# One of seven products of a SwiGLU block: high and low tokens side by side in matmuls of 512 columns, for eight of ten weight pairs

## The chip, the cores and the metric

The kernel runs on one core of a Trainium2 chip. Its engines are named as the profile names them: PE (matmuls; PEld is its weight load), DVE (VectorE), ACT (ScalarE), POOL (GpSimd) and SP (SyncE, which here issues DMAs). The metric is the device time of one execution in microseconds (us); less is better.

## The reference

One hybrid block on 512 tokens of width 1024, all in float32. A first normalisation and input product feed two token mixers (a gated convolution and a gated linear recurrence), which are merged by sigmoid gates. Then follows the channel mixer, in which the change lies:

```
h = rmsnorm(x, norm2_g[l])
x = x + (jax.nn.silu(h @ ffn_w1[l]) * (h @ ffn_w3[l])) @ ffn_w2[l]
return rmsnorm(x, norm_f_g)
```

The hidden width is 2816, so `ffn_w1` and `ffn_w3` are 1024x2816, and `ffn_w2` is 2816x1024.

## The kernel before

**Precision.** PE multiplies in a reduced format, so each float32 operand is split into a high and a low part (`split_to`, L121): ACT casts the value to the high part (L123), and DVE or POOL subtracts it from the value, which gives the low part (L119). A product is then three matmuls: high by high, high by low, low by high.

**Seven products.** For the channel mixer the tokens and the weight matrices are cut in quarters, and seven products of sums of quarters take the place of eight of quarters. The 22 column blocks of `ffn_w1` and `ffn_w3` are treated as 11 pairs `k`. Pair 0 is done plainly, pairs 1 and 2 (`FIRST`) and 3 and 4 (`NEXT`) are begun early, the others run through. In the order of `F_ORDER` (L404) a pair has the products `b11`, `t1`, `b21`, `t2`, `b22`, `t3`, and `t4` of a pair comes after `t2` of the next one; for pairs 1 to 4 `b11` and `b21` are done ahead. The token side of `t1` is called `s1`: for each of the four chunks of 128 of the contraction, the left half (`LO`, columns 0 to 255) of two tiles `hs0_0h` and `hs0_0l` and their like (the profile writes `hs_0h`, `hs_0l`).

**One product.** `f_product` (L1073) takes the weights of both matrices as eight blocks of 128x128, high and low. Matrix 1 goes to the columns `LO` of one bank of 512 columns, matrix 3 to the columns `HI` (256 to 511). Per matrix and chunk there are three matmuls of 256 columns (L1080), 24 in all.

**What follows a product.** `ffn_product` (L1169) writes `t1` to a bank `fe` out of a pool of two banks, and ACT copies it to a tile `se` in SBUF (L1185, 128x512). Later DVE adds `se` to the bank of `b22` (L906), and the product `t3` to `se`; ACT's silu (L1145) and a multiply on DVE (L1146) make the inputs `ou`, `ov` of the output product (`or`, L953). For `t2` ACT copies the running sum to a second bank first (L1180).

**The weights.** SP loads quarters of the raw weights (`f_load`, L345, two DMAs of 256 KB each, one for each matrix) into a pool of four raw buffers or into a second pool for those that sums are made in. The sums for `t1`, `t2` and `t3` are made on DVE (L357, and L119 for the difference); the one for `t4` is made by a DMA that accumulates, issued by POOL (L355). Each is then split by ACT and DVE into one of five buffers `hl_...` (a name `hl_ft` stands for `t1` to `t4`, `hl_fb` for `b11` to `b22`). Splits are put into the program four ahead of the product that uses them (`AHEAD`). SP issues in order, so a load that waits for its buffer holds all that are behind it.

**Tiles and order.** Most tiles of 128x512 come out of one set of 59 slots (`longt`, `SLOTS`). A scheduler puts the program in its order and sets the waits; PE runs its matmuls in the order of the code.

Of the kernel before, what the change touches and what calls it, by code (L numbers as in the profile page):

```python
# [8 lines left out]
F32 = mybir.dt.float32  # L9
F32R = mybir.dt.float32r  # L10
# [34 lines left out]
PLAIN, FIRST, NEXT = 0, (1, 2), (3, 4)  # L45
# [41 lines left out]
def tile_block(ctx, tc, a, out):  # L87
    nc = tc.nc
# [8 lines left out]
    def tiles(tag, bufs):  # L97
        p_ = pool(tag, bufs)
        return lambda name, dtype=F32: p_.tile([P, T], dtype, tag=tag, name=name)

    longt, shortt, gatet = tiles("long", SLOTS), tiles("short", SHORT), tiles("gate", GATES)
# [5 lines left out]
    def bank(name):  # L107
        return psum.tile([P, T], F32, tag="mm", name=name)

    def bank2(name):  # L110
        return psum2.tile([P, T], F32, tag="cv", name=name)

    vec, act, pe, pool_e = nc.vector, nc.scalar, nc.tensor, nc.gpsimd
# [66 lines left out]
    def emit_to(n, copy=act.copy, lo_by=None):  # L180
        while emitted[0] < min(len(chunks), n):
            emit_chunk(copy, lo_by)

    def weights(key, ahead=AHEAD):
        i = next(i for i, c in enumerate(chunks) if c[0] == key)
        emit_to(i + 1 + ahead)
        return held.pop(key)
# [409 lines left out]
    HALVES = [slice(0, 256), slice(256, 512)]  # L597
# [293 lines left out]
    for j in range(8):  # L891
        ws = w_tiles(f"lo{j}_0", 5) + w_tiles(f"lo{j}_1", 5)
        ps = bank(f"yb{j}")
# [12 lines left out]
    add = lambda o, x, y: vec.tensor_tensor(out=o, in0=x, in1=y, op=ALU.add)  # L906
    LO, HI = HALVES
# [99 lines left out]
    for n, j in enumerate(mixq.order()):  # L1007
        ws = w_tiles(f"co{j}", ND)
        ps = bank(f"ya{j}")
# [64 lines left out]
    def f_product(ps, k, x_, w_, again=False, ahead=AHEAD):  # L1074

        h, l = weights(f"f{w_}_{k}", ahead)
        for i in range(2):
            for c, (xh, xl) in enumerate(x_):
                for m, (lw, rx_) in enumerate(((h, xh), (h, xl), (l, xh))):
                    pe.matmul(  # L1080
                        ps[:, HALVES[i]], lw[:, 4 * i + c, :], rx_, start=not (again or i or c or m),
                        stop=bool(i and c == 3 and m == 2), skip_group_check=True,
                    )

    first = {}
    for k in FIRST:
        first[k] = bank(f"fr1_{k}"), bank(f"fr2_{k}")
# [10 lines left out]
    with tc.manual_schedule(engines={ET.PE}):  # L1098
        ws = w_tiles(f"f1_{PLAIN}", ND, 0)
        for q in range(4):  # L1100
            cs, ks = HALVES[q // 2], range(4 * (q % 2), 4 * (q % 2) + 4)
# [8 lines left out]
    f_in = {n: [] for n in ("a11", "a12", "a22", "s1", "s2", "s3", "s4")}  # L1110
# [32 lines left out]
    def f_out(c, dst, sign=1.0):  # L1143
        s_ = shortt("sl")
        act.activation(s_[:, LO], c[:, LO], AF.Silu, scale=sign)  # L1145
        vec.scalar_tensor_tensor(out=dst, in0=c[:, HI], scalar=sign, in1=s_[:, LO], op0=ALU.mult, op1=ALU.mult)  # L1146
# [15 lines left out]
    for k in NEXT:  # L1162
        f_product(first[k][1], k, f_in["a12"], "b21", True)
        o7.uv[k] = longt(f"ou{k}"), longt(f"ov{k}")
        f_out(first[k][1], o7.uv[k][0][:, LO])

    seven = {}

    def ffn_product(n, k):  # L1169

        b_ = seven.setdefault(k, {"a": first[k][0]} if k in BEGUN else {})
        x_ = {"b11": "a11", "b21": "a12", "b22": "s4", "t1": "s1", "t2": "s2", "t3": "s3", "t4": "a22"}[n]
        r = {"b11": "a", "b21": "b", "b22": "a", "t1": "e", "t2": "a", "t3": "c", "t4": "c"}[n]
        if n in ("b11", "t1"):
            b_[r] = (bank2 if r == "e" else bank)(f"f{r}_{k}")
        ps = b_[r]
        f_product(ps, k, f_in[x_], n, n not in ("b11", "t1"))
        if n in ("b11", "t2"):
            new = b_["b" if n == "b11" else "c"] = bank(f"f{n}_{k}")
            act.copy(new, ps)  # L1180
            if n == "b11":
                o7.uv[k] = longt(f"ou{k}"), longt(f"ov{k}")
        elif n == "t1":
            b_["se"] = shortt(f"se_{k}")
            act.copy(b_["se"], ps)  # L1185
        elif n == "b22":
            add(ps, ps, b_["se"])
        elif n == "t3":
            newest["added"] = add(b_["se"], ps, b_["se"]).ins
        if n not in ("b11", "t1", "t2"):  # L1190
            i, cs = {"b21": (0, LO), "b22": (0, HI), "t3": (1, HI), "t4": (1, LO)}[n]
            f_out(b_["se"] if n == "t3" else ps, o7.uv[k][i][:, cs], -1.0 if n in ("b22", "t3") else 1.0)
        if n == "t4" and k >= SUMS_FROM:
            o7.pair(k - SUMS_FROM)

    for n, k in F_ORDER:
        ffn_product(n, k)
# [93 lines left out]
```

## Time and profile before

| | |
|---|---|
| time, median of 3 runs | 797.41 us (797.23 to 797.61) |
| time of the profiled execution | 797.7 us |
| its span, first to last instruction | 795.9 us |
| granted TensorE clock | 1.000 |
| stage in which the ten pairs' products are computed | about 496 to 682 us |
| output product and end | 682 to 796 us |

The span begins with the first instruction and ends with the last, so 1.8 us of the profiled execution lie around it. A row of a timeline has a start, a duration, the engine, the line of the code, the operation, what is written and read, and in brackets how long the engine stood idle ahead of it and what ended that. Durations of DVE and ACT rows overlap the next row's start by a little; the distance of two starts is what one costs its engine. A row of a table of windows has the stretch, its length, the busy time of PE, PEld, DVE, ACT and POOL with the number of instructions, the granted clock, the busy share of the DMA engines, and GB/s. A row of waits has the waiting engine, its line, what ended the wait, the time in all, how many there were, and the longest.

### The profile page before, as it was taken

To read this page: it belongs to the slowest core of one execution; us is meant where nothing else is said; L and a number is where in the kernel's file an instruction comes from. 1 tells how busy PE (TensorE), PEld (TensorE's weight loads), DVE (VectorE), ACT (ScalarE), POOL (GpSimd) and SP (SyncE) were. 2 spreads that over 40 slices of the span, in tenths; PEclk is the share of its full clock that TensorE was granted. 3 is DMA by queue.
4 is the path that set the end of the run, shared out by engine and by line. 5 is a ranking of instruction groups with operands and counts; after the bars stand their busy time and mean duration, and the time that the engine had idled before them with its cause. 6 is when DMAs were issued, how large, how long until landed. Compare 5 with 4: busy or idle time off the path is not lost.

```text
span 795.9 us, 12177 instructions
## 1 busy us (share of the span) xinstructions
PE 789.2 (99%) x4369; PEld 690.5 (87%) x4369; DVE 673.2 (85%) x1020; ACT 471.7 (59%) x683; POOL 228.8 (29%) x181
## 2 busy tenths in 40 slices
PE   9999999999999999999999999999999999999997
PEld 8888888888888888888888898999999999888885
DVE  6699899999989988786787889978878887889757
ACT  6646585987768855563335575545455555577443
POOL 1855766797666856030000000000000000000000
PEclk9999999999999999999999999999999999999999
DMA  6945646487555664368847545566555553676652
GB/s 213 257 130 143 187 144 208 121 247 208 173 168 173 213 182 120 128 203 263 276 160 243 172 134 158 131 171 181 155 133 133 133 133 106 210 258 207 198 173 106
DMA packets 184604, 140.29 MB, mean 176 GB/s; under 512 B 14259, under 2 KB 162143, under 8 KB 184543
## 3 DMA queue, kind: packets, MB, share of 16 engines
q1 hardware_dynamic: 183103, 134.27, 55.2%
q0 software_dynamic: 1440, 5.24, 3.5%
q8 instruction: 34, 0.56, 0.3%
q14 instruction: 27, 0.22, 0.1%
HBM read 113.79 MB, written 18.64 MB: 166 GB/s over the span
## 4 chain that ended last, share of the span: by engine, by line
PE 99%; DVE 0%; issue 0%; ACT 0%
PE z L534 36%; PE or L953 13%; PE ft L1080 7%; PE yb L534 7%; PE fa L1080 7%; PE fr L1080 6%; PE ya L534 5%; PE mxr L953 5%; PE fe L1080 4%; PE g L827 3%; PE fb L1080 2%; PE f L534 2%; PE warm L506 1%; PE f L1106 1%; PE tx L574 1%; PE th L574 0%
## 5 line engine op out<-in xcount | busy, mean ns | idle before, releaser
L702 DVE SCALAR_TENSOR_TENSOR cv<-u,par,cv 128x511 f32<-128x511 f32 (+19 forms) x240 | 162.4, 730 | 5.0 <-ACT cv L699 4.7
L119 POOL TENSOR_TENSOR hl_in<-raw_in,hl_in 128x1024 fp32r<-128x1024 f32 x51 | 123.5, 2426 | 83.1 <-ACT hl_in L123 69.6
L355 POOL DMA_DIRECT2D raw_fb<-raw_fb x10 | 8.7, 874 | 298.4 <-DVE raw_fb L357 186.1
L119 POOL TENSOR_TENSOR ows<-ows 128x256 f32<-128x256 f32 x66 | 56.7, 861 | 37.7 <-DMA ows<-in_ffn_w_dram 34.7
L123 ACT CAST hl_ft<-raw_fb 128x1024 fp32r<-128x1024 f32 x40 | 41.8, 1048 | 32.5 <-DVE raw_fb L357 17.0
L123 ACT CAST hl_in<-raw_in 128x1024 fp32r<-128x1024 f32 x50 | 52.1, 1043 | 10.4 <-PE z L534 6.6
L119 DVE TENSOR_TENSOR hl_ft<-raw_fb,hl_ft 128x1024 fp32r<-128x1024 f32 x40 | 48.5, 1220 | 7.0 <-ACT hl_ft L123 6.9
L119 DVE TENSOR_TENSOR hl_fb<-raw_fb,hl_fb 128x1024 fp32r<-128x1024 f32 x30 | 36.6, 1221 | 9.5 <-ACT hl_fb L123 9.3
L357 DVE TENSOR_TENSOR raw_fb<-raw_fb,raw_fb 128x1024 f32<-128x1024 f32 x20 | 24.5, 1225 | 20.3 <-DMA raw_fb<-in_ffn_w_dram 20.0
L534 PE MATMUL z<-h10h,hl_in 128*128 128x512 f32 (+1 forms) x108 | 41.5, 385 | 0.0
L534 PE MATMUL z<-h17h,hl_in 128*128 128x512 f32 (+1 forms) x108 | 41.1, 381 | 0.0
L534 PE MATMUL z<-h13h,hl_in 128*128 128x512 f32 (+1 forms) x108 | 41.1, 381 | 0.0
L534 PE MATMUL z<-h15h,hl_in 128*128 128x512 f32 (+1 forms) x108 | 41.1, 381 | 0.0
L534 PE MATMUL z<-h14h,hl_in 128*128 128x512 f32 (+1 forms) x108 | 41.1, 381 | 0.0
L534 PE MATMUL z<-h16h,hl_in 128*128 128x512 f32 (+1 forms) x108 | 41.1, 381 | 0.0
L534 PE MATMUL z<-h12h,hl_in 128*128 128x512 f32 (+1 forms) x108 | 41.1, 381 | 0.0
L534 PE MATMUL z<-h11h,hl_in 128*128 128x512 f32 (+1 forms) x108 | 41.1, 381 | 0.0
L123 ACT CAST hl_fb<-raw_fb 128x1024 fp32r<-128x1024 f32 x30 | 31.4, 1047 | 8.9 <-PE mxr L953 3.7
L119 DVE TENSOR_TENSOR hl_ob<-raw_ob,hl_ob 128x1024 fp32r<-128x1024 f32 (+1 forms) x23 | 27.0, 1174 | 11.0 <-ACT hl_ob L123 10.9
L123 ACT CAST hl_ob<-raw_ob 128x1024 fp32r<-128x1024 f32 (+1 forms) x23 | 23.3, 1015 | 21.6 <-PE or L953 10.8
L1080 PE MATMUL fe<-hs_0h,hl_ft 128*128 128x256 f32 x160 | 30.7, 283 | 0.0
L1080 PE MATMUL ft<-hs_1h,hl_ft 128*128 128x256 f32 x160 | 30.4, 283 | 0.0
(1016 smaller groups left out, 2610.0 us busy)
## 6 DMA issues: line engine op xcount, KB each, us to landing
raw_in<-in_w_in_dram SPq DMA_DIRECT2D x52, 512.0 KB
raw_fb<-in_ffn_w_dram SPq DMA_DIRECT2D x96, 256.0 KB
ows<-in_ffn_w_dram SPq DMA_DIRECT2D x44, 256.0 KB
os<-ows SPq DMA_DIRECT2D x22, 512.0 KB
raw_ob<-in_ffn_w_dram SPq DMA_DIRECT2D x33, 256.0 KB
raw_ot<-os SPq DMA_DIRECT2D x33, 256.0 KB
raw_lo<-in_lru_w_out_dram SPq DMA_DIRECT2D x16, 320.0 KB
raw_fb<-raw_fb POOLq DMA_DIRECT2D x10, 512.0 KB, 4.6
```

Of the source, the lines that this page charges most:

```text
L119: return eng.tensor_tensor(out=o, in0=x, in1=y, op=ALU.subtract)
L123: copy(h, full)
L355: pool_e.dma_start(out=q, in_=y, accum_op=ALU.add)
L357: vec.tensor_tensor(out=q, in0=q, in1=y, op=ALU.add)
L506: pe.matmul(wp[:, :P], ones, ones, start=True, stop=True)
L534: pe.matmul(ps, l, r, start=i == 0, stop=i == n - 1)
L574: pe.transpose(ps[:, t * P : (t + 1) * P], src, ident)
L702: vec.scalar_tensor_tensor(out=acc[c][:, s:], in0=u[c][:, : T - s], scalar=dw(c, s), in1=acc[c][:, s:], op0=ALU.mult, op1=ALU.add)
L827: pe.matmul(ps, l, r, start=k == 0, stop=k == len(mms) - 1)
L953: pe.matmul(banks[i], l_[:, ts], r_, start=start and n == 0, stop=stop and n == 2, skip_group_check=again)
L1080: pe.matmul(ps[:, HALVES[i]], lw[:, 4 * i + c, :], rx_, start=not (again or i or c or m), stop=bool(i and c == 3 and m == 2), skip_group_c ...
L1106: pe.matmul(plain_1[:, cs], l, r, start=k == 0 and m == 0, stop=k == ND - 1 and m == 2)
```

## The change

A new function `f_wide` does the product `t1` of the pairs 3 to 10 (those not in `FIRST`). For it the high and the low part of `s1` are put side by side, once, in four tiles `s1b` of 512 columns, by eight DMAs from SBUF to SBUF. Each matrix has a bank of its own: a matmul of 512 columns multiplies the high weights with both parts at once, and one of 256 columns adds the low weights times the high tokens to the left half. The two halves of a bank must then be added: ACT copies the left half of each bank into its half of `se`, and DVE adds the right half.

```
+    def f_wide(banks, k, x_, both_, w_):
+
+        h, l = weights(f"f{w_}_{k}")
+        for i, ps in enumerate(banks):
+            for c, (xh, _) in enumerate(x_):
+                pe.matmul(ps, h[:, 4 * i + c, :], both_[c], start=c == 0, stop=False, skip_group_check=True)
+                pe.matmul(ps[:, LO], l[:, 4 * i + c, :], xh, start=False, stop=c == 3, skip_group_check=True)
...
+    s1_both = [longt(f"s1b{c}", F32R) for c in range(4)]
+    for both_, parts_ in zip(s1_both, f_in["s1"]):
+        for cs, v in zip(HALVES, parts_):
+            nc.sync.dma_start(both_[:, cs].bitcast(F32), v.bitcast(F32))
...
+        if n == "t1" and k not in FIRST:
+            wide = [bank2(f"fe{i}_{k}") for i in range(2)]
+            f_wide(wide, k, f_in[x_], s1_both, n)
+            b_["se"] = shortt(f"se_{k}")
+            for cs, ps in zip(HALVES, wide):
+                act.copy(b_["se"][:, cs], ps[:, LO])
+                add(b_["se"][:, cs], ps[:, HI], b_["se"][:, cs])
+            return
```

On PE the rows of `t1` of pair 3 began before with these (a name is followed by a number of its own; `x2` stands for two like rows on end; one matrix has 12 matmuls of this kind, the product 24):

```order
L1080 MATMUL fe_5172<-hs_0h,hl_ft_3_5048 128x256
L1080 MATMUL fe_5172<-hs_0l,hl_ft_3_5048 128x256
L1080 MATMUL fe_5172<-hs_0h,hl_ft_3_5048 128x256 x2
L1080 MATMUL fe_5172<-hs_0l,hl_ft_3_5048 128x256
L1080 MATMUL fe_5172<-hs_0h,hl_ft_3_5048 128x256 x2
```

In the changed kernel the same place has a first bank (5184) with eight rows and a second (5185) that begins like it:

```order
L1090 MATMUL fe_3_5184<-s1b_4868,hl_ft_3_5060 128x512
L1091 MATMUL fe_3_5184<-hs_0h,hl_ft_3_5060 128x256
L1090 MATMUL fe_3_5184<-s1b_4869,hl_ft_3_5060 128x512
L1091 MATMUL fe_3_5184<-hs_0h,hl_ft_3_5060 128x256
L1090 MATMUL fe_3_5184<-s1b_4870,hl_ft_3_5060 128x512
L1091 MATMUL fe_3_5184<-hs_0h,hl_ft_3_5060 128x256
L1090 MATMUL fe_3_5184<-s1b_4871,hl_ft_3_5060 128x512
L1091 MATMUL fe_3_5184<-hs_0h,hl_ft_3_5060 128x256
L1090 MATMUL fe_3_5185<-s1b_4868,hl_ft_3_5060 128x512
```

Twenty-four rows of 256 columns became sixteen, of 512 and 256 in turn; the products ahead and behind have the rows that they had, and so has PE everywhere else.

On SP, these are the loads of raw weights for pairs 2 and 3 before:

```order
L345 DMA raw_fb_2_4878<-in_ffn_w_dram 128x4x128 x2
L345 DMA raw_fb_2_4872<-in_ffn_w_dram 128x4x128 x2
L345 DMA raw_fb_2_4875<-in_ffn_w_dram 128x4x128 x2
L345 DMA raw_fb_3_5035<-in_ffn_w_dram 128x4x128 x2
L345 DMA raw_fb_3_5038<-in_ffn_w_dram 128x4x128 x2
```

And in the changed kernel (`raw_fb_3_5047` is the quarter `b11` of pair 3, `raw_fb_3_5050` the quarter `b12`, in which the sum is made):

```order
L345 DMA raw_fb_2_4887<-in_ffn_w_dram 128x4x128 x2
L1178 DMA s1b_4868<-hs_0h 128x256
L1178 DMA s1b_4868<-hs_0l 128x256
L1178 DMA s1b_4869<-hs_0h 128x256
L1178 DMA s1b_4869<-hs_0l 128x256
L1178 DMA s1b_4870<-hs_0h 128x256
L1178 DMA s1b_4870<-hs_0l 128x256
L1178 DMA s1b_4871<-hs_0h 128x256
L1178 DMA s1b_4871<-hs_0l 128x256
L345 DMA raw_fb_3_5047<-in_ffn_w_dram 128x4x128 x2
L345 DMA raw_fb_3_5050<-in_ffn_w_dram 128x4x128 x2
```

The eight copies stand between the last load for pair 2 and the first for pair 3; all other rows of SP keep their order.

On DVE, around `t1` of pair 5 before (`hl_fb_5` is the split for `b22` of pair 5, `hl_ft_5` that for its `t3`, `raw_fb_6` the sum for `t1` of pair 6):

```order
L1146 TENSOR_SCALAR ov_4864<-se_5367,sl 128x256
L119 TENSOR_TENSOR hl_fb_5_5539<-raw_fb_5_5404,hl_fb_5_5539 128x1024
L357 TENSOR_TENSOR raw_fb_6_5601<-raw_fb_6_5601,raw_fb_6_5598 128x1024
L119 TENSOR_TENSOR hl_ft_5_5568<-raw_fb_5_5369,hl_ft_5_5568 128x1024
L1146 TENSOR_SCALAR ou_5536<-fb_5_5534,sl 128x256
```

And in the changed kernel:

```order
L1154 TENSOR_SCALAR ov_4864<-se_5368,sl 128x256
L119 TENSOR_TENSOR hl_fb_5_5544<-raw_fb_5_5408,hl_fb_5_5544 128x1024
L906 TENSOR_TENSOR se_5563<-fe_5_5542,se_5563 128x256
L357 TENSOR_TENSOR raw_fb_6_5601<-raw_fb_6_5601,raw_fb_6_5598 128x1024
L906 TENSOR_TENSOR se_5563<-fe_5_5543,se_5563 128x256
L119 TENSOR_TENSOR hl_ft_5_5568<-raw_fb_5_5373,hl_ft_5_5568 128x1024
L1154 TENSOR_SCALAR ou_5540<-fb_5_5538,sl 128x256
```

The add of the first bank stands ahead of the next pair's sum, the add of the second ahead of the split for `t3`. Pairs 5 to 9 look like this. For pairs 3, 4 and 10 both adds stand together, behind the split for `t3` in pairs 3 and 4. In the rows of pairs 8 to 10 some rows of DVE and ACT that make the sums for the output product also change places.

## The prediction

> **What bounds the kernel now.** I read the page from the top: busy shares, the clock row, then the chain that ended last.
>
> ```profile
> PE 789.2 (99%) x4369; PEld 690.5 (87%) x4369; DVE 673.2 (85%) x1020; ACT 471.7 (59%) x683; POOL 228.8 (29%) x181
> PEclk9999999999999999999999999999999999999999
> PE 99%; DVE 0%; issue 0%; ACT 0%
> ```
>
> PE is busy for 99% of the span, at full clock in all forty slices, and it is 99% of the chain. Only work taken from PE, or a wait put in front of it, can move the end. Next I read the table of windows over the stretch in which the eight changed products lie (k = 3 to 10, from 532 to 682 us), and the waits from 505 to 690.
>
> ```profile
> 532.00:682.00 150.00, 150.00 (x1252) 150.00 (x1251) 118.47 (x151) 78.87 (x115) 6.01 (x7) 1.00 0.53 141
> DVE raw_fb L357 <- DMA raw_fb<-in_ffn_w_dram: 20.0, 9, 3.3
> PEld ft L1080 <- DVE se L906: 0.3, 1, 0.3
> PEld fr L1080 <- ACT ft L1180: 0.2, 1, 0.2
> ```
>
> In these 150 us PE is never idle. DVE is busy for 118.47, ACT for 78.87, and the DMA engines for 0.53 of the time. PE waits only twice between 505 and 690, 0.3 and 0.2 us. DVE waits 20.0 us for raw weights, so it has room too.
>
> **What a matmul costs.** The chain of waits lists whole runs of equal matmuls, so a spacing is a quotient.
>
> ```profile
> 375.34 43.52 PE ya L534 x192
> 584.10 2.88 PE fe L1080 x24
> ```
>
> 192 matmuls of 512 columns take 43.52 us: 226.7 ns each. 24 of 256 columns, one `fe` product, take 2.88 us: 120.0 ns each. Twice 120.0 is 240.0, so a pair of 256 with the same weights costs 13.3 ns more than one of 512. If a matmul is a constant plus its columns, 106.7 ns stand for 256 columns and 13.3 for the instruction. I take that reading, since 106.7 x 2 + 13.3 gives the 226.7 back.
>
> The wide product puts 512 and 256 columns in turn. The timeline has two unstalled places where the size changes:
>
> ```profile
> 458.61 0.39 PE L953 MATMUL mxr<-mxt43h,mxvb3l 128*128 128x512 f32 x1
> 458.84 0.28 PE L1080 MATMUL fr<-h20h,hl_fb 128*128 128x256 f32 x1
> 458.96 0.28 PE L1080 MATMUL fr<-h20l,hl_fb 128*128 128x256 f32 x1
> ...
> 685.66 0.28 PE L1080 MATMUL ft<-h27h,hl_ft 128*128 128x256 f32 x1
> 685.78 0.40 PE L953 MATMUL or<-hl_ob,ous0h 128*128 128x512 f32 x1
> ```
>
> From 512 to 256 the starts are 0.23 apart, from 256 to 256 and from 256 to 512 0.12: no extra cost for the change of size, to the 10 ns of this column.
>
> [...]
>
> **PE's part of the change.** Per product 24 x 120.0 = 2.88 us become 8 x 226.7 + 8 x 120.0 = 2.77 us: 0.107 us less. There are eight products: **0.85 us** (64 x 13.3 ns). PE's order is otherwise the same.
>
> **The eight copies on SP.** Each fills 128x256 of a long tile from `hs_0h` or `hs_0l`. They stand behind the loads for k = 2 and ahead of those for k = 3. The rows below are from SP's timeline, the waits of its queue, the page's list of DMA issues, a table of windows, and DVE's timeline.
>
> ```profile
> 67.85 0.54 SPq L807 DMA_DIRECT2D ext1h<-xb2h  x1
> 69.72 0.60 SPq L807 DMA_DIRECT2D ext3l<-xb2l  x1
> SPq L345 <- DMA raw_fb<-raw_fb: 10.2, 1, 10.2
> raw_fb<-raw_fb POOLq DMA_DIRECT2D x10, 512.0 KB, 4.6
> 505.00:511.00 6.00, 6.00 (x53) 6.00 (x52) 4.41 (x7) 1.99 (x4) 0.00 (x0) 1.00 0.88 260
> 511.00:515.00 4.00, 4.00 (x34) 3.83 (x33) 3.93 (x4) 2.50 (x4) 0.86 (x1) 1.00 0.03 8
> 515.00:518.50 3.50, 3.50 (x31) 3.50 (x31) 3.50 (x5) 1.52 (x3) 0.00 (x0) 1.00 0.79 150
> 522.15 1.23 DVE L357 TENSOR_TENSOR raw_fb<-raw_fb,raw_fb 128x1024 f32<-128x1024 f32 x1 [2.85 <-DMA raw_fb<-in_ffn_w_dram]
> ```
>
> Issuing: the existing copies of one tile into another, of the same 128 KB, hold SP 0.54 to 0.60 us each (four from 67.85 to 70.32, 0.62 apart), so eight take about 5 us. The `b11` loads of k = 3, which are among those of the first window, go that much later, and SP comes to its wait at 513 instead of 508. The queue had nothing else to do: SP waits 10.2 us at that place (508 to 518) for POOL's accumulating DMA. Transfer: 8 x 128 KB = 1.05 MB. At the 260 GB/s at a share of 0.88 of the first window (295 at full share) that is 3.6 us of all DMA engines. The DMA engines stood at 0.03 from 511 to 515, which is 3.9 us of room. So the copies and the moved load fit, by a little, ahead of the accumulate, which moves 512 KB from 515 to 518.5 and whose landing releases the next load. The moved load itself is a summand of the sum that DVE starts at 522.15, several microseconds behind its landing. The first wide product starts at 532.1, some 18 us after the copies land. Cost between nothing and the full 3.6 us of delay on the weights for k = 3 and 4; I take nothing, and the second rival prices the rest.
>
> **ACT and DVE.** One ACT copy of 128x512 becomes two of 128x256 and two DVE adds of 128x256. Their timelines around k = 5:
>
> ```profile
> 566.85 0.59 ACT L1185 COPY se<-fe 128x512 f32<-128x512 f32 x1 [0.73 <-PE fe L1080]
> 563.47 0.68 DVE L906 TENSOR_TENSOR se<-ft,se 128x512 f32<-128x512 f32 x1
> 564.06 0.42 DVE L119 TENSOR_TENSOR oe<-ou,ov 128x256 f32<-128x256 f32 x1
> 564.40 1.22 DVE L119 TENSOR_TENSOR hl_ft<-raw_fb,hl_ft 128x1024 fp32r<-128x1024 f32 x1
> 570.34 1.23 DVE L357 TENSOR_TENSOR raw_fb<-raw_fb,raw_fb 128x1024 f32<-128x1024 f32 x1 [2.97 <-DMA raw_fb<-in_ffn_w_dram]
> 574.17 1.22 DVE L119 TENSOR_TENSOR hl_ft<-raw_fb,hl_ft 128x1024 fp32r<-128x1024 f32 x1
> ```
>
> ACT's pass over 512 columns takes 0.59 us, so two over 256 take between 0.59 and 1.18; I take 0.7, as on DVE two passes over 256 (0.34 each, below) cost a little more than one over 512 (0.59), and ACT has 71 idle us in the window for eight times the difference. By the next start, a DVE pass over 256 takes 0.34; no add of this shape from PSUM to SBUF stands in the trace, so it is bounded by 0.34 and by 0.59, the 512 add (563.47 to 564.06). I take 0.34: 0.68 us per pair, 5.4 us in all, on an engine with 31 idle us in the window. For k = 5 to 9 the first add stands ahead of the next pair's sum. At k = 5 that sum waits 2.97 us for its load until 570.34, and the add can run at about 567.5: hidden. The second delays the split behind it by 0.34. The weights for `t1` of k = 6 are begun at 574.17 and done at 575.4, and PE reads them at 584.10, so 0.7 us on DVE are covered by 8.7. Without that cover PE would lose all of them, 5.4 us.
>
> For k = 3 and 4 both adds stand behind the `t3` split. Here the cover is thinnest:
>
> ```profile
> 537.50 1.23 DVE L357 TENSOR_TENSOR raw_fb<-raw_fb,raw_fb 128x1024 f32<-128x1024 f32 x1 [3.26 <-DMA raw_fb<-in_ffn_w_dram]
> 538.80 1.05 ACT L123 CAST hl_ft<-raw_fb 128x1024 fp32r<-128x1024 f32 x1 [3.04 <-DVE raw_fb L357]
> 539.76 0.58 ACT L1180 COPY ft<-fr 128x512 f32<-128x512 f32 x1
> 540.73 0.28 PE L1080 MATMUL fr<-hs_1h,hl_fb 128*128 128x256 f32 x1
> 538.98 2.36 DVE L119 TENSOR_TENSOR hl_ft<-raw_fb,hl_ft 128x1024 fp32r<-128x1024 f32 x2
> 546.49 0.28 PE L1080 MATMUL fe<-hs_0h,hl_ft 128*128 128x256 f32 x1
> ```
>
> The sum for k = 4 waits 3.26 us for its load, ACT's cast waits for the sum, and the copy that frees `fr` for `b22` of k = 3 is queued behind the cast. It ends at 540.34, PE needs it at 540.73: 0.39 us of cover, of which the faster product eats 0.11. No add comes ahead of this. The two adds of k = 3 go between the two splits from 538.98, the second of which is for `t1` of k = 4: it ends at 542.0 instead of 541.3, and PE reads it from 546.5 on. In the tail (k = 8 to 10) four more long slots are held and DVE's rows change places, one `ov` write now behind `b11` of k = 10 on PE; the split for `b22` of k = 10 shows the cover there:
>
> ```profile
> 666.34 1.23 DVE L119 TENSOR_TENSOR hl_fb<-raw_fb,hl_fb 128x1024 fp32r<-128x1024 f32 x1 [0.96 <-ACT hl_fb L123]
> 676.09 0.28 PE L1080 MATMUL fa<-hs_1h,hl_fb 128*128 128x256 f32 x1
> ```
>
> It is done at 667.6 and read from 676.09: 8.5 us, and I charge nothing. The output stage is started by PE's last `t4`, so the gain passes through.
>
> **The sum.** The profiled execution took 797.7 us, a span of 795.9 and 1.8 around it. 797.7 - 0.85 = 796.85. The median of the runs shown is 797.41, 0.3 lower, so on that scale **796.6 us**, 0.11% less. A measurement of this kernel tells about 0.2% from no change: 1.6 us, so "faster" is under 795.8 and "slower" over 799.0.
>
> **Rivals.** 1) *The 13.3 ns are not the instruction's.* If they go with columns, or if alternating two output widths pays them back, the products stay at 2.88 us: 797.3 to 797.5. For it speaks that no run in the trace alternates unstalled. Against it stand the two changes of size above. That the change doesn't do what it says comes out at the same time.
>
> 2) *Slower: the copies delay the weights of k = 3 and 4.* Should they collide with the accumulate by x us, the load behind it, the sum at 537.50, the cast and the copy that frees `fr` all come x later, and PE waits x - 0.28 at 540.73. It breaks even with the gain at x = 1.1; it is slower by over 0.2% from x = 2.7 (2.4 lost against 0.85 gained). With all of the 3.6 us serial it is 796.6 + 3.3 = 799.9. For it: the sums at 522.15 and 537.50 both end waits for their loads, so a delay of the loads reaches them whole. Against it: the hole of 3.9 us, at the same place.
>
> 3) *Slower: alternation stalls.* There is one place where 512 and 256 alternate:
>
> ```profile
> 477.36 0.40 PE L534 MATMUL f<-h20l,hl_f 128*128 128x512 f32 x1
> 477.59 0.38 PE L1106 MATMUL f<-h26h,hl_f 128*128 128x256 f32 x1
> 477.80 0.39 PE L534 MATMUL f<-h21h,hl_f 128*128 128x512 f32 x1
> 478.04 0.39 PE L1106 MATMUL f<-h26l,hl_f 128*128 128x256 f32 x1
> ```
>
> Here a 256 is followed only after 0.21 instead of 0.12. At 64 places that would be 64 x 0.09 = 5.8 us lost: 802.3. But those 256s read `h26h` and `h26l` just as they are made (their 0.38 and 0.39 against 0.28 elsewhere shows the wait), which the wide product's inputs are not.
>
> **How the numbers follow.** Forecast (0.85 gained, all else hidden): 0.66, 796.2 to 797.0. Rival 1, or a collision that eats the gain: 0.21, 797.0 to 799.0. Rivals 2 and 3 beyond 0.2%: 0.05 and 0.05. More than forecast: 0.03. The range runs from 796.2 to 798.0: 0.4 below for run-to-run spread, above past the case without gain. Faster by over 0.2% needs 1.6 us where PE's whole saving is 0.85: 0.03. Within: 0.87. Slower: 0.10.
>
> **What would show it.** Right: a wide product in the chain takes 2.77 us, 2.88 now; PE busy all through the window 532 to 682; `ft` on ACT still ends before PE's `b22` of k = 3; DVE's adds last near 0.4 us each. Wrong: 2.88 us (rival 1), 256s followed after 0.2 us (rival 3), or a wait of PE between 520 and 545 with a late accumulate (rival 2).

## The result, and the profile after

The changed kernel is slower by a little: 798.93 us (median of 20 runs) against 797.73 us for the kernel before (20 runs), a ratio of 1.0014 (1.0008 to 1.0021). The forecast was 796.6, within 796.2 to 798.0. The profiled execution took 797.99 us, with a span of 796.2.

The page's rows that answer to those of before: PE has 64 matmuls less and is busy for 1.4 us less, but it is no longer 99% of the chain that ended last.

```profile
PE 787.8 (99%) x4305; PEld 685.8 (86%) x4305; DVE 678.4 (85%) x1036; ACT 472.1 (59%) x691; POOL 229.3 (29%) x181
PE 96%; DMA 1%; DVE 1%; ACT 1%; issue 0%; SPq 0%; DVEq 0%; ACTq 0%
```

The table of windows, for the stage of the products and for the 53 us that follow, in which the output stage begins; the last row is the kernel before:

```profile
532.00:682.00 150.00, 150.00 (x1188) 146.72 (x1187) 124.68 (x169) 79.74 (x124) 6.02 (x7) 1.00 0.53 142
682.00:735.00 53.00, 52.15 (x241) 43.13 (x240) 48.08 (x79) 36.98 (x57) 0.00 (x0) 1.00 0.71 229
...
682.00:735.00 53.00, 53.00 (x245) 43.79 (x244) 48.87 (x80) 37.51 (x56) 0.00 (x0) 1.00 0.68 232
```

In the first row PE is still never idle, and DVE carries 6.2 us more (5.4 forecast). The second row is new: PE stands idle for 0.85 us in the output stage, where the kernel before had none (53.00 busy of 53.00). The chain of waits through one wide product, and its end:

```profile
532.00 0.23 PE fe L1090
532.23 0.12 PE fe L1091
532.35 0.24 PE fe L1090
...
534.71 0.12 PE fe L1091
534.83 2.87 PE fr L1080 x24
```

From 532.00 to 534.83 are 2.83 us: 0.05 less than the 2.88 of before, where 0.107 was forecast. Eight of them save 0.40 us. And the chain through the output stage, which in the kernel before is one run of PE from 685.94 on:

```profile
682.32 3.00 PE ft L1080 x24
685.32 34.20 PE or L953 x151
...
722.75 4.06 DMA raw_ot<-os
...
726.91 1.05 ACT hl_ot L123
...
732.68 0.61 DVE x2b L906
733.30 0.04 issue
733.34 57.27 PE or L953 x250
```

The chain leaves PE for a load of weights, `raw_ot`, that lands late. ACT's cast waits for it, the splits on DVE follow, and DVE's add of `x2b`, on which PE's next bank waits, comes behind them. ACT's timeline has two such places, of the kernel before:

```profile
702.76 1.05 ACT L123 CAST hl_ob<-raw_ob 128x1024 fp32r<-128x1024 f32 x1 [1.46 <-DMA raw_ob<-in_ffn_w_dram]
726.24 1.06 ACT L123 CAST hl_ot<-raw_ot 128x1024 fp32r<-128x1024 f32 x1 [0.64 <-DVE ov L119]
```

and of the changed one:

```profile
703.08 1.05 ACT L123 CAST hl_ob<-raw_ob 128x1024 fp32r<-128x1024 f32 x1 [2.40 <-DMA raw_ob<-in_ffn_w_dram]
726.91 1.05 ACT L123 CAST hl_ot<-raw_ot 128x1024 fp32r<-128x1024 f32 x1 [1.94 <-DMA raw_ot<-os]
```

PE came to the output stage 0.6 us sooner, and at 703 a load ate that up: the cast stands 0.3 us later, not 0.6 sooner. At 726 another 0.7 is lost, of which DVE keeps 0.3. In the kernel before, DVE is busy for all of the 31.00 us from 704 to 735, so there is no slack in it to make up for either.

Two lengths serve below. The **product stage** runs from the first of `fr` x96 to the first `or` behind the last `t4`: 459.00 to 685.94 before (226.9 us), 458.76 to 685.32 after (226.6). The **output stage** runs from there to the end of the span: 110.0 before, 110.9 after.

### The profile page after: what moved, and what is told of

It is laid out like the page before. It is cut to its first block, busy times and chain, and to the rows that moved or that the text cites. A ratio compares the mean times of both kernels' runs of the same rounds, so it can differ in the third digit from the quotient of the medians.

```text
span 796.2 us, 12091 instructions
## 1 busy us (share of the span) xinstructions
PE 787.8 (99%) x4305; PEld 685.8 (86%) x4305; DVE 678.4 (85%) x1036; ACT 472.1 (59%) x691; POOL 229.3 (29%) x181
## 4 chain that ended last, share of the span: by engine, by line
PE 96%; DMA 1%; DVE 1%; ACT 1%; issue 0%; SPq 0%; DVEq 0%; ACTq 0%
PE z L534 36%; PE or L953 12%; PE ft L1080 7%; PE yb L534 7%; PE fa L1080 7%; PE fr L1080 6%; PE ya L534 5%; PE mxr L953 5%; PE g L827 3%; PE fb L1080 2%; PE f L534 2%; PE fe L1090 2%; PE fe L1091 1%; PE f L1114 1%; PE fe L1080 1%; DMA x<-in_x_dram 1%
## 5 line engine op out<-in xcount | busy, mean ns | idle before, releaser
L119 DVE TENSOR_TENSOR hl_fb<-raw_fb,hl_fb 128x1024 fp32r<-128x1024 f32 x30 | 36.6, 1221 | 6.4 <-ACT hl_fb L123 6.3
L123 ACT CAST hl_ot<-raw_ot 128x1024 fp32r<-128x1024 f32 (+1 forms) x17 | 17.5, 1029 | 20.1 <-PE or L953 10.2
```

Of the source, the lines that this page charges most:

```text
L119: return eng.tensor_tensor(out=o, in0=x, in1=y, op=ALU.subtract)
L123: copy(h, full)
```

## The experiments

Theory 1 was that the output stage is paced by its loads, so that nothing gained on PE arrives; theory 2, that the copies and the four tiles held longer cost the time (2a the DMAs, 2b the tiles); theory 3, that the added passes on DVE do.

**A saving on PE alone** (kernel before):

```
+                    if w_ == "t1" and 3 <= k <= 9 and (i, c, m) == (1, 2, 1):
+                        continue
```

> The kernel before, with one of the 24 matmuls of 256 columns left out in the product t1 of seven pairs (part of one low-token term is missing): 7 x 120 ns = 0.84 us less on PE and nothing else changed, about what the forecast was to gain. Theory 1 (the output stage is paced by its loads and by DVE, so PE arriving earlier only waits longer): 797.5 to 797.9, and the wait of PE for x2b in the output stage grows by about 0.8 us. Rival (a saving on PE passes to the end): 0.84 us less, about 796.9.

Measured: 796.92 us, ratio 0.999 (0.9982 to 0.9999). The product stage took 226.1 us and the output stage 109.9. Theory 1 falls: 0.84 us less on PE arrive at the end (0.75 us less at the median than the 797.67 of the kernel before beside it).

**Copies and tiles without the wide product** (changed kernel; `t1` as before, reading `s1b`):

```
+            f_in["s1b"] = [(v[:, LO], v[:, HI]) for v in s1_both]
+            x_ = "s1b"
+        if False:
```

> The copies and the four tiles s1b of the changed kernel, but t1 done as before in 24 matmuls of 256 columns, now reading s1b. No wide matmul, no added DVE pass. Theory 2 (four more held tiles and the eight DMAs, with the changed order of DVE's rows in pairs 8 to 10, cost the time): about 1 us or more over before, 798.7 to 799.5. Theory 1 alone, or theory 3 (the added DVE passes cost it): as before, 797.4 to 798.0.

Measured: 798.57 us, ratio 1.0008 (1.0000 to 1.0017). The output stage is that of before (109.9), the product stage took 227.7. Its chain from 513 on, and PE's waits from 505 to 690:

```profile
513.75 6.37 DMA raw_fb<-raw_fb
...
520.58 3.31 DMA raw_fb<-in_ffn_w_dram
...
524.01 1.24 DVE raw_fb L357
...
525.32 1.05 ACT hl_ft L123
526.37 0.49 ACT ft L1204
...
526.91 3.14 PE fr L1080 x24
```

```profile
PEld fr L1080 <- ACT ft L1204: 0.7, 2, 0.5
PE fr L1080 <- ACT ft L1204: 0.3, 1, 0.3
```

This is the second rival of the prediction, one pair sooner than it was placed: the accumulating DMA takes 6.4 us instead of 4.6, and the load behind it, the sum, the cast and the copy that frees `fr` follow, here for `b22` of pair 2. What it collides with shows in the row of windows for 511 to 515, which had a DMA share of 0.03 before:

```profile
511.00:515.00 4.00, 4.00 (x33) 3.85 (x33) 3.93 (x4) 2.50 (x4) 0.87 (x1) 1.00 0.75 231
```

POOL issues the accumulate at 513.75, and from 514 to 515 the DMA engines still carry 333 GB/s, the moved load, where the kernel before moves nothing.

**The same with the copies on POOL:**

```
-            nc.sync.dma_start(both_[:, cs].bitcast(F32), v.bitcast(F32))
+            pool_e.tensor_copy(out=both_[:, cs], in_=v.bitcast(F32))
```

> The kernel that has the copies and the four tiles but no wide product (it took 798.6), with the copies made by POOL, not by DMA. Theory 2a (the eight DMAs delay the loads of pairs 3 and 4, and PE waits for ft): 797.4 to 797.9. Theory 2b (four more held tiles cost it): 798.3 to 798.8 again.

Measured: 797.68 us, ratio 1.0001 (0.9992 to 1.0010), product stage 226.9. The wait for `ft` is gone from the trace. So it is the DMAs (2a), although the intervals of the two runs overlap and the trace has to decide; the tiles and the changed order of DVE's rows in pairs 8 to 10 cost nothing that shows.

**The wide product without the adds:**

```
-                add(b_["se"][:, cs], ps[:, HI], b_["se"][:, cs])
```

> The changed kernel without the 16 DVE adds (the high weights times the low tokens are left out of t1). Theory 3 (the adds cost the time): 797.3 to 797.8. Theory 2: still 798.6 to 799.2.

Measured: 798.53 us, ratio 1.0004 (0.9995 to 1.0012): not told apart from either kernel by the time. In its trace the output stage takes 111.4 us without any of the adds, so theory 3 does not explain that loss.

**The wide product without copies and tiles** (each part of the split written to its place):

```
+            b1, b2 = pairt(f"hs{k}_0")
+            for b, cs in ((b1, LO), (b2, HI)):
+                split_to(b[:, LO], b[:, HI], g[0][:, cs], vec)
...
```

> The wide product of the changed kernel without copies and without further tiles: the split of s1 and s2 writes high and low side by side at once. Order in pairs 8 to 10 as before, the added DVE passes stay. Theory 2: the loss goes, and what remains is the PE saving seen in the trace, 0.4 us, so 797.2 to 797.7. Theory 1 alone: the same 797.7, with PE waiting longer in the output stage. Theory 3: still about 1 us slower than before, 798.7.

Measured: 800.08 us, ratio 1.0030 (1.0019 to 1.0040), outside all three. The smaller splits changed DVE's order in pairs 1 and 2, and the products wait for weights there (PEld 1.0 us and PE 0.8 for `hl_ft` from DVE); ahead of `b22` of pair 3 they wait for `ft` from ACT (0.6 and 0.4). The output stage took 111.6. The run is of no use for the product stage, but its trace shows that the loss in the output stage needs neither the copies nor the tiles.

The kernels with the wide product had a long output stage, the others not. What they share is 64 matmuls less ahead of it. The DMA view has a queue `q8` of the kind "instruction": 34 packets of 16 KB (0.56 MB) over the span, before as after. Its rows in the changed kernel, in windows from 694 to 698, from 720 to 725 and from 721.8 to 722.0 (packets, MB, share of 16 engines' time):

```profile
q8 instruction: 1, 0.02, 1.5%
q8 instruction: 1, 0.02, 36.6%
```

The first row stands for either of the first two windows. 36.6% of 16 times 0.2 us is 1.17 us: so long the packet is under way, from 721.9. In the kernel before, neither window has a row of `q8`; there the piece lies between 707 and 712:

```profile
q8 instruction: 1, 0.02, 1.7%
```

In the kernel before the pieces come 14.6 to 16.2 us apart between 532 and 682, with 123 to 135 matmuls of PE begun from one to the next, and 24 to 30 us apart behind 685, with 108 to 133. The one at 709.0 comes when PE has begun 4014 matmuls, the one at 721.9 in the changed kernel when it has begun 4009. So the pieces go with PE's instructions and not with the time, and I take them for PE's code: 64 matmuls less put them half a distance later in the work. The piece at 696 lies in the burst of loads ahead of the cast at 703, the one at 722 on the loads of `raw_ot`, whose issue takes SP longer in the changed kernel:

```profile
722.39 1.04 SPq L274 DMA_DIRECT2D raw_ot<-os  x2
```

than in the kernel before:

```profile
722.39 0.80 SPq L274 DMA_DIRECT2D raw_ot<-os  x2
```

Theory 4 is that the moved pieces of PE's code make the loss in the output stage; by what step a piece would hold up a load, no run here shows.

**The changed kernel, and the kernel before, with 64 more matmuls at the start:**

```
-WARM = 21
+WARM = 6
...
+    for _ in range(94):
+        pe.matmul(wp[:8, :8], onesr[:, :8], onesr[:, :8], start=True, stop=True)
```

> The changed kernel with 64 more matmuls on PE in the warm-up at the start (the warm-up has 6 of the old and 94 tiny ones, to take no longer), so that PE's stream again has as many instructions ahead of the output stage as before. Theory 4 (PE's code comes in pieces of 16 KB by DMA; the changed kernel has 64 matmuls less, so a piece now falls on the weights raw_ot of the output stage and holds them up): the pieces stand near 709 and 739 us again, PE no longer waits 2.4 us for x2b, and the time is 797.3 or less. Rival (the two output banks, or the DVE passes, make the output stage late): still 798.5 to 799.2.

> The kernel before with the same 64 more matmuls in the warm-up and nothing else. Theory 4: a piece of PE's code now falls near 722 us, as in the changed kernel, PE waits for x2b, and the time rises by about 1 us, to 798.5 to 799. Rival: 797.4 to 798.0, as before.

Measured: 801.0 us (1.0038, 1.0025 to 1.0051) and 801.8 us (1.0056, 1.0043 to 1.0069). As times both miss, since the edit costs some 3 us earlier: PE waits for its first inputs, and a piece that now comes at 508 lies beside the loads of pairs 1 and 2 (PEld waits 1.0 us there, PE 0.8, for `hl_ft`). The order on DVE, ACT, POOL and SP is row for row that without the edit. The output stages answer as theory 4 has it: 109.9 with the wide product and the piece at 712, 24 us into the stage (in the kernel before 23); 111.0 in the kernel before with the piece at 725.5, 37 us into it (in the changed kernel 36). These are one trace each. PE's waits there, of the kernel before with the longer warm-up:

```profile
PEld or L955 <- DVE x2b L908: 1.6, 2, 1.4
PE or L955 <- DVE x2b L908: 0.9, 1, 0.9
```

And of the changed kernel with it:

```profile
PEld or L955 <- DVE x2b L908: 0.5, 2, 0.3
```

**The order within a bank** (changed kernel, longer warm-up):

```
+            for c in range(4):
+                pe.matmul(ps, h[:, 4 * i + c, :], both_[c], ...)
             for c, (xh, _) in enumerate(x_):
-                pe.matmul(ps, h[:, 4 * i + c, :], both_[c], ...)
                 pe.matmul(ps[:, LO], l[:, 4 * i + c, :], xh, ...)
```

> As the changed kernel with the longer warm-up, but in each bank the four matmuls of 512 columns come first and then the four of 256, so that the size changes once in a bank and not seven times. If a change of size costs (the wide product took 2.83 us, not 2.77): 2.78 us for a product, 0.3 to 0.4 us less than with the alternation. If the 512-column matmuls on two-part tokens are themselves dearer: 2.83 again.

Measured: 800.23 us (1.0034, 1.0022 to 1.0047). One product in its chain:

```profile
566.49 0.93 PE fe L1092 x4
567.42 0.47 PE fe L1094 x4
567.89 0.93 PE fe L1092 x4
568.82 0.48 PE fe L1094 x4
569.29 0.12 PE fb L1082
```

2.80 us against 2.83 alternated and 2.77 forecast, between the two expectations. So about half of the missing saving goes with the order. The rest is in the short runs of 512 columns: 0.93 for four is 232 ns each, not 226.7. That is not peculiar to `s1b`, for in the kernel before the four `or` that stand between products of 256 columns take as long, and 458 of them on end only 227.9 ns each:

```profile
682.01 0.93 PE or L953 x4
685.94 104.37 PE or L953 x458
```

Whether a short run pays at the change of size on either side or in its own matmuls, these rows do not separate.

**Copies on POOL, in two kernels with the wide product** (the edit as above):

> As the changed kernel with the longer warm-up, but the eight copies are made by POOL and not by DMA. If the eight DMAs sometimes delay the loads of pairs 3 and 4 (PE waited 1 us for ft in the run that had only copies and tiles): less than the changed kernel with the longer warm-up by up to 0.8 us. If they do not in that kernel: the same within 0.3 us.

> The changed kernel with the copies made by POOL. Theory 4 leaves the loss of about 1 us in the output stage, against 0.4 gained on PE: 798.0 to 798.5. If theory 2a holds also for the changed kernel, it is under the changed kernel's 798.9 by 0.3 to 0.8. If the DMAs are the whole cause: 797.3.

Measured: 800.97 us with the longer warm-up (1.0043, 1.0029 to 1.0056), and 798.58 without it (1.0013, 1.0004 to 1.0022). The first is that of the copies by DMA (801.0), so they delay nothing there that shows. The second has a product stage of 227.0 us, no wait of PE for `ft`, and an output stage of 111.0; the 0.4 us that PE's matmuls save does not show in its product stage either. Taking the DMAs away does not heal the kernel, as theory 4 has it; whether it helps by 0.3 us isn't told apart.

**The wide product in half of the pairs**, as it stands, and with both mends:

```
-        if n == "t1" and k not in FIRST:
+        if n == "t1" and k in (3, 4, 5, 6):
```

> The changed kernel with the wide product in pairs 3 to 6 only (32 matmuls less, not 64); 7 to 10 as before. Theory 4: the pieces of PE's code come a quarter of a piece later than before, near 30 and 61 us after the last t4 begins its last matmul, not on raw_ot at 37; the output stage takes 110.2 us from that matmul again, and the time is 797.3 to 798.0. Rival (a loss in proportion to the wide products): half of what the changed kernel loses, 798.3, with an output stage of about 110.7.

> Wide product in pairs 3 to 6 only, the four matmuls of 512 columns ahead of the four of 256 in each bank, copies by POOL. A product took 2.81 us in that order, 0.07 less than before, so four save 0.29. If the piece of PE's code and the DMAs are the two causes, neither is left: 797.2 to 797.6, the only form so far that is not slower than before. If there is a third cause: 798 or more.

Measured: 798.03 us (1.0004, 0.9995 to 1.0013) and 797.77 us (1.0005, 0.9996 to 1.0013). With the piece 30 and 32 us into the output stage, this takes 109.9 and 110.0, as theory 4 has it. But the second time lies between its two expectations, the product stages took 227.4 and 227.1, so that the saving of 0.2 to 0.3 us does not arrive, and neither kernel beats the one before.

**The changed kernel, three executions more:**

> The changed kernel unchanged, one more profiled execution. The profiled one lost 0.95 us in the output stage and won 0.39 on PE, which leaves some 0.6 of the median's 1.2 open. If the eight DMAs delay the loads of pairs 3 and 4 in some executions (theory 2a), such an execution shows PE waiting 0.3 to 1 us for ft at about 526, and an accumulating DMA of over 5.8 us; if not, the product stage is as in the first trace and the output stage takes more than 111 us.

> As the run before: the same kernel, another execution, to see how often PE waits for ft at about 526 and how far the length of the output stage varies (110.9 in the first trace; up to 111.6 in other kernels with the piece of code at the same place).

> As the two before, a third execution: the median's missing 0.6 us is found if at least two of the three show either the wait at 526 or an output stage of 111.3 us or more.

Measured, one execution each: 797.51, 798.31 and 799.22 us; the kernel before took 798.82 in its one run beside them. Product stages: 226.7, 227.9 and 227.8 us; output stages: 110.0, 110.0 and 110.4. PE's waits of the second, from 505 to 690:

```profile
PEld fr L1080 <- ACT ft L1201: 1.3, 2, 1.1
PE fr L1080 <- ACT ft L1201: 0.9, 1, 0.9
```

In the third PE waits 0.6 us for `ft`, in the first not at all. Both waits stand at 541, ahead of `b22` of pair 3, where the prediction's second rival has them, and not at 526. The chain of the third:

```profile
535.25 3.52 DMA raw_fb<-in_ffn_w_dram
...
538.89 1.24 DVE raw_fb L357
...
541.24 0.50 ACT ft L1201
541.74 0.04 issue
541.78 3.14 PE fr L1080 x24
```

The accumulating DMA issued at 513 took 5.8, 5.6 and 5.8 us in the three, and the next one, issued at 528 to 529, 4.7, 6.0 and 5.5. And with the pieces of code at the same places, the output stage lost 0, 0 and 0.4: a piece there can cost something, but need not.

## Why the prediction was wrong

**What bounds the kernel: right.** PE sets the time, and a saving on it arrives at the end (the run with seven matmuls left out: 0.84 us less on PE, 0.75 less at the median).

**What a matmul costs: right in kind, half in size.** The step that failed was "no extra cost for the change of size, to the 10 ns of this column". The 7 ns that a pair of 512 and 256 takes above 346.7 (2.83 us are eight pairs of 353.7) lie under that resolution, and 64 of them are 0.45 us. With it failed the price of 226.7 ns, which was read from 192 matmuls on end and does not hold for one or four between others. The term "0.85 us (64 x 13.3 ns)" measured 0.40.

**The copies: the step "I take nothing" failed.** The second rival's chain is right link by link. What was wrong is that "the copies and the moved load fit, by a little, ahead of the accumulate". SP issues a copy every 0.67 us (506.10 to 511.49 in the changed kernel) and the moved load behind them; they take up most of the hole (a share of 0.75 from 511 to 515 in the run with copies and tiles, 0.03 before), and its end too. The accumulate issued at 513 to 515 took 5.4 to 6.4 us in the seven traces that have the copies by DMA and the old warm-up, and 4.6 to 5.1 in the six that have no such copies. In the two with the longer warm-up it starts 2.8 to 2.9 us behind the issue of the moved load, not 1.7 to 1.9, and takes 4.6. Alone the copies cost 0.9 us at the medians (798.57 against 797.68 with the copies on POOL). In the changed kernel PE waits for `ft` in two of four traces; the profiled execution, which has no such wait, could not tell. There the next accumulate, at 528 to 529, comes in too, and its length is not the copies' doing: it took 4.7 to 6.0 us with and without them, 5.6 in the kernel before.

**ACT, DVE and the tail: right.** ACT's two copies take 0.64 us instead of 0.59; an add on DVE takes 0.42 as a row and 0.34 to the next start where two stand on end (539.90 to 540.57), as forecast; and without the adds nothing was won in the stage that lost; the changed order of pairs 8 to 10 costs nothing that shows (copies on POOL without the wide product).

**"The output stage is started by PE's last `t4`, so the gain passes through": this failed, and no rival held it.** The start passes through, but 64 matmuls less move the pieces of PE's code against the work, and in the profiled execution two (at 695.8 and 721.9) fall beside loads behind which DVE, busy without a pause in the kernel before, has no slack. In nine traces with the piece elsewhere (23 to 25, or 30 to 32 us into the stage) the stage took 109.9 to 110.1. In eight with it at 36 to 37 it took 110.0 twice, 110.4 once and 110.9 to 111.6 five times.

**The sum.** Over the four traces of the changed kernel the product stage is 226.6, 226.7, 227.9 and 227.8 against 226.9, on the mean 0.3 more; the output stage 110.9, 110.0, 110.0 and 110.4 against 110.0, on the mean 0.4 more. That is 0.7 of the 1.2 us, whose interval is 0.6 to 1.7; three of the four executions lie under the median of 798.93, and where the rest goes stays open. So does what decides in an execution whether the two collisions happen: with the same work ahead of it, the product stage begins anywhere from 457.99 to 459.30 in the traces with the old warm-up. Apart from all this, 0.3 us of the distance to the forecast is its scale, the median of three runs (797.41, where twenty gave 797.73). That a piece of code holds up a load beside it is my inference from the packet's times (1.17 us from 721.9, the load of `raw_ot` from 722.75), and no run shows how; that moving the pieces moves the loss is shown by the pair with the longer warm-up, one trace each, and borne out by the seventeen traces above.

## What to carry to other kernels

Here PE was busy for 99% and DVE followed without slack, and taking 64 matmuls out of PE also moved the pieces of its code, from 23 to 36 us into the output stage: look up the queue of the kind "instruction" in the DMA view before and after, and what its packets fall on. A hole in the DMA share that a burst fills "by a little" was no cover: 3.6 us of copies in a hole of 3.9 us brought the transfer behind them from 4.6 to 5.1 us up to 5.4 to 6.4. And a saving of some nanoseconds per instruction needs a price read from a run of the very pattern, since the timeline's last digit (10 ns) was as large as the gain (13.3 ns forecast for a pair, 6 measured).

## What was not expected of the hardware

What I take for PE's code comes by DMA in packets of 16 KB: 34 for the 4369 pairs of weight load and matmul of the kernel before, where PE begins 108 to 144 matmuls from one to the next (127 on the mean). Each lasts there 0.9 to 2.0 us (1.0 in the middle), as long as a third of a load of 256 KB takes to land here (3.3 us for `raw_fb` in the run with copies and tiles).
